# Head norms as one broadcast product, norm weights folded into rotary tables and splits

## The chip, the cores and the metric

The kernel runs on one core of a Trainium2 chip. The metric is the device time of one execution in microseconds; the figure for a kernel is the median of its runs. Besides the runs, one execution is recorded by the hardware profiler; its span runs from the first to the last instruction of the program. The core's engines are PE (matrix products), DVE (vector), ACT (scalar), POOL (GpSimd) and SP, which here only issues DMAs. Each engine executes its instructions strictly in the order in which the program lists them, and waits for others by semaphores.

## The reference

Two layers, each on 512 tokens of width 1024. A layer norms its input, multiplies it by one wide matrix, and hands the columns to four groups; their outputs are gated, joined, multiplied by `w_out` and added to the input. The change concerns two of the groups. In the first (latent attention) queries and keys come from low-rank projections that are themselves normed, and each head is normed again:

```
q = (rmsnorm(cq, mla_q_norm_g) @ mla_w_uq).reshape(B, S, MLA_HEADS, MLA_QK)
kv = (rmsnorm(ckv, mla_kv_norm_g) @ mla_w_ukv).reshape(B, S, MLA_HEADS, MLA_NOPE + MLA_V)
k_nope, v_a = kv[..., :MLA_NOPE], kv[..., MLA_NOPE:]
q = rmsnorm(q, mla_q_g)
q = jnp.concatenate([q[..., :MLA_NOPE], rope(q[..., MLA_NOPE:], positions)], axis=-1)
k_nope = rmsnorm(k_nope, mla_k_nope_g)
k_rope = rope(rmsnorm(kr, mla_k_rope_g)[:, :, None, :], positions)
```

There are 4 heads of 96 channels: 64 without position (`nope`), then 32 rotated ones. The ranks are 256 (`cq`) and 128 (`ckv`). In the second (block attention) both `mq` and `mk` are 4 heads of 64 channels, normed per head with `moba_q_g` and `moba_k_g`; their first 16 channels are rotated. A norm is `x * rsqrt(mean(x*x) + eps) * g`, a rotation is

```
x1, x2 = xf[..., :half], xf[..., half:]
return jnp.concatenate([x1 * cos - x2 * sin, x2 * cos + x1 * sin], axis=-1)
```

Both attentions use scores `q . k * scale` (scale 96^-0.5 and 64^-0.5) and a causal softmax.

## The kernel before

All products run in a form of float32 split in two: an operand is written as a rounded `hi` and the rest `lo` (`split2`, line 249: ACT copies `hi`, DVE subtracts to get `lo`), and a product is three matmuls (`mm3`, line 254). Tokens are four tiles of 128 rows.

The order of instructions on each engine is made by a planner in the kernel's own text (`Order`, line 67, and `Chain`, line 151). Every piece of work is a coroutine; each emitted instruction advances a clock of its engine by a cost formula, and the coroutine whose inputs come first by these clocks emits next. PE's clock is the planner's time. So a change of any instruction's cost or engine can move other instructions in the queues. The planner knows some DMAs (`dma`, line 262) and not others (the small parameter loads). `Slots` (line 113) hand out buffers; a coroutine waits for a free one.

What runs over what: `main` (line 1320), at the lowest priority, fills PE with the wide projection, first `cq` (the 416 columns of `cq`, `ckv`, `kr`) for the four tiles, then the units of `SEQ` (line 338) in order (`sq` with the columns of mq, then `ga`, `kv` with those of mk, `su`, `gc` and so on), and at last the output projection. Weights come in units: `load_units` (line 360) issues their loads on SP, `split_units` (line 378) splits each in two halves when PE is about to want it or when ACT and DVE are idle; it gives `hi` to DVE where ACT's clock is 600 ns ahead of DVE's.

The steps that the change and the prediction touch:

- `load_params` (line 528) loads 13 small parameter arrays of a layer on SP, each gain copied to all 128 partitions (`bcast`, line 511); its `scale` multiplies two of them on POOL by minus the score scale. For layer 0 it is called when the load of `ukv` has been issued (line 1536), for layer 1 from `next_params` (line 1265).
- `rope_tables` (line 445) computes cosine and sine of the positions on DVE or POOL, whichever is idle by the planner's clocks, at low priority, and sets `rope_ev`.
- `low_chain` (line 680), per tile: DVE multiplies the projected rows `a` by the low-rank gains `cg` into `ct` (line 687), PE transposes `ct` (`cT`), it is split (`cTh`, `cTl`), and PE forms `q` and `kv`. `low_stats` (line 650) takes the sums of squares on ACT meanwhile.
- `q_chain` (line 714) and `kv_chain` (line 743): copy to `Q` or `K`, four squares on ACT, POOL's power, then four DVE products, one per head, of rows times the head's factor times the gain; then Q is rotated (`rope`, line 635: six products and sums, on DVE or POOL, with one scratch tile `rb` for all rotations, so that these follow one another).
- `mqk_chain` (line 980) does the same for `mq` and `mk`.
- `mla_heads` (line 1132) starts when all tiles of `Q` and `K` are ready: per head PE transposes Q (`t0a`) and K (`t1a`), each is split (`hi0a`, `lo0a`, `hi1a`, `lo1a`), then scores, softmax, and product with V. `moba_heads` (line 1174) follows with pairs of heads (`mq0d`, `mk0d`, `kl0d` and so on).
- `sv_chain` (line 776) norms `vn`, which `mix_chain` (line 800) multiplies on PE (`mp`).
- `t_sums` (line 318) adds weight blocks in memory for the output projection by accumulating DMAs that POOL issues.

Of the kernel before, what the change touches and what calls it, by code (L numbers as in the profile page):

```python
# [11 lines left out]
F32 = mybir.dt.float32  # L12
# [188 lines left out]
def hybrid_trunk(ctx: ExitStack, tc: tile.TileContext, x, positions, norm_g, w_c, w_f, w_t, w_o, mla_q_norm_g,  # L201
# [176 lines left out]
    def split_units():  # L378
        for u in order:
# [3 lines left out]
            n = u.a * u.b  # L383
            for i in range(2):
# [142 lines left out]

    def load_params(L):
        l = L.l
        L.cg = lay.tile([P, 384], F32, tag="cg_b", name="cg_b")  # L530
        nc.sync.dma_start(L.cg[:, 0:256], dram(mla_q_norm_g, l * 256, [[0, P], [1, 256]]))
        nc.sync.dma_start(L.cg[:, 256:384], dram(mla_kv_norm_g, l * 128, [[0, P], [1, 128]]))
        L.gq = bcast(mla_q_g, l * 96, 96, "gq_b")
        L.gk = bcast(mla_k_nope_g, l * 64, 64, "gk_b")
# [3 lines left out]
        L.dq = bcast(moba_q_g, l * 64, 64, "dq_b")  # L538
        L.dk = bcast(moba_k_g, l * 64, 64, "dk_b")
# [8 lines left out]

        def scale():
            ch = Chain(o, L.par_t)  # L550
            yield from ch.pool(G.tensor_scalar, L.gq, L.gq, -(96 ** -0.5), None, op0=ALU.mult)
            yield from ch.pool(G.tensor_scalar, L.dq, L.dq, -0.125, None, op0=ALU.mult)
# [3 lines left out]
    for l in range(DEPTH):  # L556
        L = Layer()
        L.l = l
        L.ng_ev = Event()
# [75 lines left out]
    def rope(ch, x1, x2, cb, sb, nh, nd, name):  # L635
# [5 lines left out]
        for out_, in0, in1, op in ((ta, x2, sb, ALU.mult), (tb, x1, sb, ALU.mult), (x1, x1, cb, ALU.mult),  # L641
                                   (x2, x2, cb, ALU.mult), (x1, x1, ta, ALU.subtract), (x2, x2, tb, ALU.add)):
# [7 lines left out]
    def low_stats(L, t, a, t0, done):  # L650
# [24 lines left out]
        yield from rope(ch, krt[:, :, 0:16], krt[:, :, 16:32], cosT, sinT, 4, 16, f"k{L.l}")  # L675
# [4 lines left out]
    def low_chain(L, t, a, t0):  # L680
# [6 lines left out]
        yield from ch.dve(V.tensor_tensor, ct[:, :384], a[:, :384], L.cg, op=ALU.mult)  # L687
# [26 lines left out]
    def q_chain(L, t, q_ps, t0):  # L714
# [19 lines left out]
        for h in range(4):  # L734
            yield from ch.dve(V.scalar_tensor_tensor, Q[:, t, h, :], in0=Q[:, t, h, :], scalar=m[:, 4 + h:5 + h],
                              in1=L.gq, op0=ALU.mult, op1=ALU.mult)
        yield from ch.wait(rope_ev)
# [880 lines left out]
```

## Time and profile before

| | before |
|---|---|
| median of 3 runs | 497.65 us (497.48 to 499.13) |
| the profiled execution | 499.12 us, span 497.4 us |
| PE busy | 486.4 us, 98% of the span |
| DVE busy | 386.0 us, 78% |
| ACT busy | 317.0 us, 64% |
| POOL busy | 156.2 us, 31% |

Times in the profile are microseconds from the start of the span, unless they are marked or known as nanoseconds (mean time of one instruction of a group). A group is a line of the kernel, an engine, an operation, and output and input tiles with buffer numbers left out; as nearly all instructions are recorded at the planner's line 162 or 188, one goes by the tiles. After the bar stand busy time, mean of one, idle time of the engine just before, and what ended it. PE's instructions overlap, so the busy time of PE includes the end of one under the next; a 128x512 matmul follows the one before it after 0.23 us though it lasts 0.39.

### The profile page before, as it was taken

Reading aid. Unit: us, or ns where it says so; the run is one execution under the profiler, and the core shown is the slowest. Engines: PE = TensorE matmul, PEld = TensorE weight load, DVE = VectorE, ACT = ScalarE, POOL = GpSimd, SP = SyncE. Lnnn points to the kernel's source line nnn. Section 1 sums busy time; section 2 is a strip of 40 time slices with the busy share of each in tenths; the row PEclk is TensorE's granted clock in tenths of the full one; section 3 lists DMA queues with packets and bytes.
Section 4 is the critical chain, followed back from the end, with each engine's and each line's share of the span. In section 5 each row is a group of like instructions: output and inputs, shape, how many; then the busy total and the mean of one; then the engine's idle time right before and its main releaser. Section 6 shows DMA issues by size and latency. Waiting matters only on the chain.

```text
span 497.4 us, 7832 instructions
## 1 busy us (share of the span) xinstructions
PE 486.4 (98%) x2448; PEld 412.5 (83%) x2448; DVE 386.0 (78%) x1008; ACT 317.0 (64%) x933; POOL 156.2 (31%) x328
## 2 busy tenths in 40 slices
PE   6899999999999999999999999999999999999997
PEld 4798878788888888888889988888888888888886
DVE  4877884777988788669898698677969788765992
ACT  5688753576777775446657896567758587524640
POOL 6867883656110000000031388463351000000000
PEclk9999999999999999999999999999999999999999
DMA  8545559444575235786474232664548528565642
GB/s 273 150 141 199 196 117 203 171 86 88 192 145 188 71 98 175 210 299 219 157 256 157 86 106 108 211 149 97 118 122 245 142 102 215 174 249 188 227 171 92
DMA packets 35339, 81.98 MB, mean 165 GB/s; under 512 B 7137, under 2 KB 16609, under 8 KB 35042
## 3 DMA queue, kind: packets, MB, share of 16 engines
q1 hardware_dynamic: 26818, 73.10, 42.7%
q0 software_dynamic: 8480, 8.39, 11.5%
q8 instruction: 19, 0.31, 0.3%
q14 instruction: 22, 0.18, 0.1%
HBM read 73.61 MB, written 24.64 MB: 198 GB/s over the span
## 4 chain that ended last, share of the span: by engine, by line
PE 87%; POOL 4%; ACT 3%; DMA 3%; DVE 2%; issue 1%; POOLq 0%; DVEq 0%
PE kv L188 7%; PE cq L188 6%; PE oy L188 6%; PE sq L188 5%; PE cb L188 4%; PE gd L188 4%; PE ch L188 4%; PE cc L188 4%; PE su L188 4%; PE gc L188 4%; PE gb L188 4%; PE ox L188 4%; PE oz L188 4%; PE sa L188 3%; PE ga L188 2%; PE od L188 2%
## 5 line engine op out<-in xcount | busy, mean ns | idle before, releaser
L162 ACT ACTIVATE pd<-pd,mnd 128x256 f32<-128x256 f32 (+3 forms) x50 | 26.9, 547 | 2.8 <-DVE mnd L162 2.3
L330 POOL DMA_DIRECT2D t<-in_w_o_dram x16 | 17.9, 1121 | 33.1 <-DMA t<-t 22.6
L162 ACT ACTIVATE pha<-pTa 128x512 fp32r<-128x512 f32 (+3 forms) x32 | 13.9, 436 | 20.0 <-PE pTa L188 19.8
L188 PE MATMUL kv<-whi_kv,hTh 128*128 128x512 f32 x64 | 26.1, 408 | 0.0
L188 PE MATMUL kv<-whi_kv,hTl 128*128 128x512 f32 x64 | 25.1, 392 | 0.0
L188 PE MATMUL kv<-wlo_kv,hTh 128*128 128x512 f32 x64 | 25.0, 391 | 0.0
L188 PE MATMUL cq<-whi_c,hTh 128*128 128x416 f32 x64 | 24.0, 376 | 0.0
L162 ACT ACTIVATE phd<-pTd 128x512 fp32r<-128x512 f32 (+3 forms) x32 | 13.8, 434 | 14.9 <-PE pTd L188 14.7
L162 ACT ACTIVATE pa<-pa,mna 128x256 f32<-128x256 f32 (+3 forms) x40 | 21.4, 542 | 2.5 <-DVE mna L162 2.4
L188 PE MATMUL cq<-whi_c,hTl 128*128 128x416 f32 x64 | 22.6, 353 | 0.0
L188 PE MATMUL cq<-wlo_c,hTh 128*128 128x416 f32 x64 | 22.5, 351 | 0.0
L162 DVE TENSOR_TENSOR wlo_t<-raw_t,whi_t 128x512 fp32r<-128x512 f32 x32 | 21.1, 691 | 0.0
L162 ACT ACTIVATE whi_t<-raw_t 128x512 fp32r<-128x512 f32 x32 | 18.2, 618 | 4.1 <-DMA raw_t<-t 4.1
L162 POOL TENSOR_SCALAR xss<-xss 128x1 f32<-128x1 f32 x8 | 3.8, 476 | 52.3 <-ACT jk L162 45.1
L162 DVE TENSOR_TENSOR pla<-pTa,pha 128x512 fp32r<-128x512 f32 (+3 forms) x32 | 15.2, 484 | 5.5 <-ACT pha L162 5.5
L188 PE MATMUL sq<-yTh,hTh 128*128 128x512 f32 x48 | 18.9, 393 | 0.0
L188 PE MATMUL sq<-yTh,hTl 128*128 128x512 f32 x48 | 18.7, 390 | 0.0
L162 DVE TENSOR_TENSOR pld<-pTd,phd 128x512 fp32r<-128x512 f32 (+3 forms) x32 | 15.2, 484 | 4.5 <-ACT phd L162 4.4
L188 PE MATMUL sq<-yTl,hTh 128*128 128x512 f32 x48 | 18.7, 390 | 0.0
L162 DVE CUSTOM_DVE_ANT_0 pa<-sa,maskb 128x512 f32<-128x512 f32 (+3 forms) x32 | 14.8, 484 | 5.0 <-PE pTa L188 4.2
L162 DVE TENSOR_TENSOR wlo_b<-raw_b,whi_b 128x512 fp32r<-128x512 f32 x24 | 16.0, 688 | 0.7 <-ACT whi_b L162 0.7
L162 DVE CUSTOM_DVE_ANT_0 pd<-sd,maskb 128x256 f32<-128x256 f32 (+3 forms) x32 | 15.0, 483 | 2.0 <-PE pTd L188 1.9
(377 smaller groups left out, 1853.0 us busy)
## 6 DMA issues: line engine op xcount, KB each, us to landing
t<-in_w_o_dram POOLq DMA_DIRECT2D x16, 512.0 KB, 6.2
raw_t<-t SPq DMA_DIRECT2D x16, 512.0 KB, 4.0
raw_b<-in_w_o_dram SPq DMA_DIRECT2D x12, 512.0 KB, 4.2
raw_sq<-in_w_t_dram SPq DMA_DIRECT2D x8, 512.0 KB, 3.5
t<-in_w_o_dram SPq DMA_DIRECT2D x8, 512.0 KB, 4.4
raw_kv<-in_w_t_dram SPq DMA_DIRECT2D x8, 512.0 KB, 3.6
t<-t SPq DMA_DIRECT2D x8, 512.0 KB, 4.8
ys<-ysc SPq DMA_DIRECT2D x14, 256.0 KB, 5.2
```

Of the source, the lines that this page charges most:

```text
L162: f(*a, **k)
L188: f(*a, **k)
L330: nc.gpsimd.dma_start(z_src(l, n, j), quad(l, b, j), accum_op=ALU.add, max_dma_last_dim=1024)
```

## The change

- The four per-head products of each tile in `q_chain`, `kv_chain` and `mqk_chain` become one DVE product of the tile with the four factors, each repeated along its head; the gain is no longer in it.
- The gains of rotated channels go into four tables per kind (`tables`: cosine and sine times the gain of either half), made on POOL once per layer for Q, mq and mk. Rotation waits for its own table (`tab_ev`) in place of `rope_ev`.
- The gains of the other channels, of q and k together, and minus the score scale become one column per head dimension (`kac`, `kdc`), by which ACT and DVE multiply when transposed k is split. The split waits for `col_ev`.
- The low-rank gains become columns `cg`, applied where `uq` and `ukv` are split; those splits wait for `cg_ev`, and `hi` is always made on ACT. `ct` becomes a plain copy on ACT.
- `load_low_gain` issues the two loads of `cg`, in layer 0 right after the load of `c3` and ahead of the third and fourth tile of x. With them a layer has 18 small loads where it had 13 (six copied to all partitions for nine, six new ones of 64 numbers each).

```diff
@@ -381,6 +381,9 @@
             n = u.a * u.b
+            low = u.name[:-2] in ("uq", "ukv")
+            if low:
+                yield from ch.wait(layers[int(u.name[-1])].cg_ev)
             for i in range(2):
@@ -389,6 +392,13 @@
                 hi, lo, raw = u.hi[:, sl], u.lo[:, sl], u.raw[:, sl]
+                if low:
+                    k = i if u.a == 2 else 2
+                    col = layers[int(u.name[-1])].cg[:, k:k + 1]
+                    yield from c2.act(A.activation, hi, raw, AF.Copy, scale=col)
+                    yield from c2.dve(V.scalar_tensor_tensor, lo, in0=raw, scalar=col, in1=hi.bitcast(F32),
+                                      op0=ALU.mult, op1=ALU.subtract)
+                    continue
                 if o.clk["V"] + 600.0 < o.clk["A"]:
@@ -525,18 +535,29 @@
+    def load_low_gain(L):
+        L.cg = lay.tile([P, 4], F32, tag="cg", name="cg")
+        nc.sync.dma_start(L.cg[:, 0:2], dram(mla_q_norm_g, L.l * 256, [[1, P], [P, 2]]))
+        nc.sync.dma_start(L.cg[:, 2:3], dram(mla_kv_norm_g, L.l * P, [[1, P], [1, 1]]))
+        o.set(L.cg_ev, o.now + 4000.0)
+
     def load_params(L):
         l = L.l
-        L.cg = lay.tile([P, 384], F32, tag="cg_b", name="cg_b")
-        nc.sync.dma_start(L.cg[:, 0:256], dram(mla_q_norm_g, l * 256, [[0, P], [1, 256]]))
-        nc.sync.dma_start(L.cg[:, 256:384], dram(mla_kv_norm_g, l * 128, [[0, P], [1, 128]]))
-        L.gq = bcast(mla_q_g, l * 96, 96, "gq_b")
-        L.gk = bcast(mla_k_nope_g, l * 64, 64, "gk_b")
+        if l:
+            load_low_gain(L)
+        gq = bcast(mla_q_g, l * 96 + 64, 32, "gq_b")
         L.gr = bcast(mla_k_rope_g, l * 32, 32, "gr_b")
...
         L.lb = bcast(sg_ln_b, l * GW, GW, "lb_b")
-        L.dq = bcast(moba_q_g, l * 64, 64, "dq_b")
-        L.dk = bcast(moba_k_g, l * 64, 64, "dk_b")
+        dq = bcast(moba_q_g, l * 64, 16, "dq_b")
+        dk = bcast(moba_k_g, l * 64, 16, "dk_b")
+        L.ka = lay.tile([P, 2], F32, tag="ka", name="ka")
+        L.kd_ = lay.tile([P, 2], F32, tag="kd", name="kd")
+        for i, (a, b) in enumerate(((mla_q_g, moba_q_g), (mla_k_nope_g, moba_k_g))):
+            n = (96, 64)[i]
+            nc.sync.dma_start(L.ka[0:64, i:i + 1], dram(a, l * n, [[1, 64], [1, 1]]))
+            for r in range(2):
+                nc.sync.dma_start(L.kd_[r * 64:r * 64 + 64, i:i + 1], dram(b, l * 64, [[1, 64], [1, 1]]))
         L.sgb = lay.tile([P, 4], F32, tag="sgb", name="sgb")
@@ -546,17 +567,41 @@
+        def tables(ch, g, cs, sn, n, nm):
+
+            tab = lay.tile([P, 4, NT, n], F32, tag=f"tb{nm}", name=f"tb{nm}{l}")
+            for i, (w, h) in enumerate(((cs, 0), (sn, 1), (cs, 1), (sn, 0))):
+                yield from ch.pool(G.tensor_tensor, tab[:, i], w,
+                                   g[:, h * n:(h + 1) * n].unsqueeze(1).to_broadcast([P, NT, n]), op=ALU.mult)
+            L.tab[nm] = tab
+            o.set(L.tab_ev[nm], ch.t)
+
         def scale():
+
             ch = Chain(o, L.par_t)
-            yield from ch.pool(G.tensor_scalar, L.gq, L.gq, -(96 ** -0.5), None, op0=ALU.mult)
-            yield from ch.pool(G.tensor_scalar, L.dq, L.dq, -0.125, None, op0=ALU.mult)
+            yield from ch.wait(rope_ev)
+            yield from tables(ch, gq, cosT, sinT, 16, "q")
+            ce, se = (z.rearrange("p t (i two) -> p t i two", two=2)[:, :, :, 0] for z in (cosT, sinT))
+            yield from tables(ch, dq, ce, se, 8, "mq")
+            yield from tables(ch, dk, ce, se, 8, "mk")
+            L.kac = lay.tile([P, 1], F32, tag="kac", name="kac")
+            L.kdc = lay.tile([P, 1], F32, tag="kdc", name="kdc")
+            yield from ch.pool(G.memset, L.kac[64:96, :], -(96 ** -0.5))
+            yield from ch.pool(G.tensor_scalar, L.kac[0:64, :], L.ka[0:64, 0:1], L.ka[0:64, 1:2], -(96 ** -0.5),
+                               op0=ALU.mult, op1=ALU.mult)
+            yield from ch.pool(G.tensor_scalar, L.kdc, L.kd_[:, 0:1], L.kd_[:, 1:2], -0.125,
+                               op0=ALU.mult, op1=ALU.mult)
+            for r in (0, 64):
+                yield from ch.pool(G.memset, L.kdc[r:r + 16, :], -0.125)
+            o.set(L.col_ev, ch.t)
         o.spawn(scale(), None if L.l else MIXT, 2)
...
         L.l = l
-        L.ng_ev = Event()
+        L.ng_ev, L.cg_ev = Event(), Event()
+        L.tab, L.tab_ev, L.col_ev = {}, {n: Event() for n in ("q", "mq", "mk")}, Event()
         L.hT = [[Event(), Event()] for _ in range(NT)]
@@ -632,14 +677,14 @@
-    def rope(ch, x1, x2, cb, sb, nh, nd, name):
+    def rope(ch, x1, x2, c1, s2, c2, s1, nh, nd, name):
         tab = yield from rbS.get(ch, f"rb{name}")
...
         on_dve = o.clk["V"] + ROPEB < max(o.clk["G"], ch.t)
-        for out_, in0, in1, op in ((ta, x2, sb, ALU.mult), (tb, x1, sb, ALU.mult), (x1, x1, cb, ALU.mult),
-                                   (x2, x2, cb, ALU.mult), (x1, x1, ta, ALU.subtract), (x2, x2, tb, ALU.add)):
+        for out_, in0, in1, op in ((ta, x2, s2, ALU.mult), (tb, x1, s1, ALU.mult), (x1, x1, c1, ALU.mult),
+                                   (x2, x2, c2, ALU.mult), (x1, x1, ta, ALU.subtract), (x2, x2, tb, ALU.add)):
             if on_dve:
@@ -672,7 +717,7 @@
         yield from ch.wait(rope_ev)
-        yield from rope(ch, krt[:, :, 0:16], krt[:, :, 16:32], cosT, sinT, 4, 16, f"k{L.l}")
+        yield from rope(ch, krt[:, :, 0:16], krt[:, :, 16:32], cosT, sinT, cosT, sinT, 4, 16, f"k{L.l}")
         yield from ch.wait(L.QK_ev)
@@ -684,7 +729,7 @@
         o.spawn(low_stats(L, t, a, t0, done))
-        yield from ch.dve(V.tensor_tensor, ct[:, :384], a[:, :384], L.cg, op=ALU.mult)
+        yield from ch.act(A.activation, ct[:, :384], a[:, :384], AF.Copy)
         done(ch)
@@ -731,13 +776,11 @@
         yield from pow_rstd(ch, m[:, 4:8], m[:, 0:4], 4)
-        for h in range(4):
-            yield from ch.dve(V.scalar_tensor_tensor, Q[:, t, h, :], in0=Q[:, t, h, :], scalar=m[:, 4 + h:5 + h],
-                              in1=L.gq, op0=ALU.mult, op1=ALU.mult)
-        yield from ch.wait(rope_ev)
-        cb = cosT[:, t, :].unsqueeze(1).to_broadcast([P, 4, 16])
-        sb = sinT[:, t, :].unsqueeze(1).to_broadcast([P, 4, 16])
-        yield from rope(ch, Q[:, t, :, 64:80], Q[:, t, :, 80:96], cb, sb, 4, 16, f"q{t}{l}")
+        yield from ch.dve(V.tensor_tensor, Q[:, t], Q[:, t], m[:, 4:8].unsqueeze(2).to_broadcast([P, 4, 96]),
+                          op=ALU.mult)
+        yield from ch.wait(L.tab_ev["q"])
+        tabs = [L.tab["q"][:, i, t, :].unsqueeze(1).to_broadcast([P, 4, 16]) for i in range(4)]
+        yield from rope(ch, Q[:, t, :, 64:80], Q[:, t, :, 80:96], *tabs, 4, 16, f"q{t}{l}")
         o.set(L.qd[t], ch.t)
@@ -767,9 +810,8 @@
         yield from pow_rstd(ch, m[:, 4:8], m[:, 0:4], 4)
-        for h in range(4):
-            yield from ch.dve(V.scalar_tensor_tensor, K[:, t, h, 0:64], in0=K[:, t, h, 0:64],
-                              scalar=m[:, 4 + h:5 + h], in1=L.gk, op0=ALU.mult, op1=ALU.mult)
+        yield from ch.dve(V.tensor_tensor, K[:, t, :, 0:64], K[:, t, :, 0:64],
+                          m[:, 4:8].unsqueeze(2).to_broadcast([P, 4, 64]), op=ALU.mult)
         o.set(L.kd[t], max(ch.t, tv))
@@ -981,7 +1023,6 @@
             l = L.l
-            gn = L.dq if nm == "mq" else L.dk
             if t == 0:
@@ -995,14 +1036,11 @@
             yield from pow_rstd(ch, m[:, 4:8], m[:, 0:4], 4)
-            for h in range(4):
-                yield from ch.dve(V.scalar_tensor_tensor, dst[:, t, h, :], in0=dst[:, t, h, :],
-                                  scalar=m[:, 4 + h:5 + h], in1=gn, op0=ALU.mult, op1=ALU.mult)
-            yield from ch.wait(rope_ev)
-            ce = cosT[:, t, :].rearrange("p (i two) -> p i two", two=2)[:, :, 0]
-            se = sinT[:, t, :].rearrange("p (i two) -> p i two", two=2)[:, :, 0]
-            yield from rope(ch, dst[:, t, :, 0:8], dst[:, t, :, 8:16], ce.unsqueeze(1).to_broadcast([P, 4, 8]),
-                            se.unsqueeze(1).to_broadcast([P, 4, 8]), 4, 8, f"{nm}{t}{l}")
+            yield from ch.dve(V.tensor_tensor, dst[:, t], dst[:, t],
+                              m[:, 4:8].unsqueeze(2).to_broadcast([P, 4, 64]), op=ALU.mult)
+            yield from ch.wait(L.tab_ev[nm])
+            tabs = [L.tab[nm][:, i, t, :].unsqueeze(1).to_broadcast([P, 4, 8]) for i in range(4)]
+            yield from rope(ch, dst[:, t, :, 0:8], dst[:, t, :, 8:16], *tabs, 4, 8, f"{nm}{t}{l}")
             o.set(L.md_ev[nm][t], ch.t)
@@ -1149,7 +1187,14 @@
                 lo = yield from t2S.get(ch, f"lo{i}{H.name}", F32R)
-                yield from split2(ch, hi[:96], lo[:96], tp[:96])
+                if i == 0:
+                    yield from split2(ch, hi[:96], lo[:96], tp[:96])
+                else:
+                    yield from ch.wait(L.col_ev)
+                    col = L.kac[:96, :]
+                    yield from ch.act(A.activation, hi[:96], tp[:96], AF.Copy, scale=col)
+                    yield from ch.dve(V.scalar_tensor_tensor, lo[:96], in0=tp[:96], scalar=col,
+                                      in1=hi[:96].bitcast(F32), op0=ALU.mult, op1=ALU.subtract)
                 trS.put(ch)
@@ -1204,12 +1249,17 @@
                         pair[kind, x] = w
-                        yield from ch.act(A.activation, w[a0:a1, :], tp[a0:a1, :], AF.Copy)
-                        lo = w[b0:b1, :] if kind == "mq" else kl[a0:a1, :]
-                        if kind == "mk":
-                            yield from ch.act(A.activation, w[b0:b1, :], tp[a0:a1, :], AF.Copy)
-                        yield from ch.dve(V.tensor_tensor, lo, tp[a0:a1, :], w[a0:a1, :].bitcast(F32),
-                                          op=ALU.subtract)
+                        if kind == "mq":
+                            yield from ch.act(A.activation, w[a0:a1, :], tp[a0:a1, :], AF.Copy)
+                            yield from ch.dve(V.tensor_tensor, w[b0:b1, :], tp[a0:a1, :], w[a0:a1, :].bitcast(F32),
+                                              op=ALU.subtract)
+                        else:
+                            yield from ch.wait(L.col_ev)
+                            col = L.kdc[a0:a1, :]
+                            for r in (slice(a0, a1), slice(b0, b1)):
+                                yield from ch.act(A.activation, w[r, :], tp[a0:a1, :], AF.Copy, scale=col)
+                            yield from ch.dve(V.scalar_tensor_tensor, kl[a0:a1, :], in0=tp[a0:a1, :], scalar=col,
+                                              in1=w[a0:a1, :].bitcast(F32), op0=ALU.mult, op1=ALU.subtract)
                         o.set(pair["ev", x][0 if kind == "mq" else 1], ch.t)
@@ -1532,7 +1582,7 @@
         LOAD_HOOKS["c0_0"] = (after(1),)
-        LOAD_HOOKS["c3_0"] = (after(2), after(3))
+        LOAD_HOOKS["c3_0"] = (after(2), after(3), lambda: load_low_gain(L0))
         LOAD_HOOKS["ukv_0"] = (lambda: load_params(L0),)
...
         o.spawn(load_units(), None, 4)
```

## The prediction

> **What bounds the kernel now.** I read the sums first, then the chain that ended last, then busy time by stage.
>
> ```profile
> span 497.4 us, 7832 instructions
> PE 486.4 (98%) x2448; PEld 412.5 (83%) x2448; DVE 386.0 (78%) x1008; ACT 317.0 (64%) x933; POOL 156.2 (31%) x328
> PE 87%; POOL 4%; ACT 3%; DMA 3%; DVE 2%; issue 1%; POOLq 0%; DVEq 0%
> ```
>
> PE works 98% of the span and makes 87% of the chain. The change alters no matmul and no transpose, so it can win only where PE stands still, and lose only by making PE stand still. By stage (columns: length, busy time of PE, PEld, DVE, ACT, POOL with counts, clock, DMA share, GB/s):
>
> ```profile
> 12.50:25.00 12.50, 10.56 (x61) 9.54 (x60) 10.30 (x22) 8.47 (x27) 10.66 (x24) 1.00 0.54 153
> 25.00:37.50 12.50, 12.50 (x75) 11.91 (x74) 9.49 (x25) 10.93 (x41) 8.30 (x16) 1.00 0.44 137
> 37.50:50.00 12.50, 12.50 (x62) 10.91 (x61) 9.69 (x35) 10.91 (x51) 9.92 (x14) 1.00 0.50 201
> 62.50:75.00 12.50, 12.15 (x58) 9.82 (x58) 10.83 (x37) 7.45 (x28) 11.11 (x21) 1.00 0.53 108
> 87.50:100.00 12.50, 11.37 (x57) 9.39 (x56) 9.16 (x33) 6.70 (x30) 8.08 (x22) 1.00 0.46 169
> 275.00:287.50 12.50, 12.50 (x66) 11.35 (x66) 8.88 (x30) 10.94 (x54) 5.84 (x8) 1.00 0.23 84
> 287.50:300.00 12.50, 12.50 (x57) 10.43 (x57) 12.00 (x45) 11.70 (x55) 10.85 (x18) 1.00 0.41 128
> 487.50:497.40 9.90, 6.44 (x40) 5.64 (x38) 2.83 (x5) 0.00 (x0) 0.00 (x0) 0.98 0.26 95
> ```
>
> PE's idle time is 497.4 - 486.4 = 11.0 us. The rows hold 1.94 of it up to 25, 0.35 before 75, 1.13 before 100 and 3.46 at the end; in the slices left out PE is busy throughout but in the first, where the other 4.1 lie. The first and the last are loading, the norm of the first rows, and the last store; the change touches none of their steps. What it can reach:
>
> ```profile
> 20.20 0.34 PE L188 MATMUL cq<-whi_c,hTl 128*128 128x416 f32 x1
> 21.19 0.55 PE L188 MATMUL cT<-ident,ct 128*128 128x128 f32 x3 [0.64 <-DVE ct L162]
> 21.79 0.66 PE L188 MATMUL hT<-ident,h 128*128 128x128 f32 x4
> 71.36 0.38 PE L188 MATMUL mp<-vnh,wsh 128*128 128x256 f32 x1 [0.27 <-ACT vnh L162]
> 93.97 0.32 PE L188 MATMUL t0a<-ident,Q 128*96 128x128 f32 x1 [1.13 <-DVE Q L162]
> ```
>
> That is 0.64 + 0.35 (0.27 and 0.08 behind it) + 1.13 = **2.1 us**, the most that can be won. The other 1.3 us before 25 belong to the norm of the second 128 rows, untouched.
>
> **Head norms.** The four products per tile and the multiplication of `ct`, in all uses of both layers, then rows for what replaces them:
>
> ```profile
> L162 DVE SCALAR_TENSOR_TENSOR Q<-Q,mq,gq_b 128x96 f32<-128x96 f32 x32 | 10.2, 320 | 0.0
> L162 DVE SCALAR_TENSOR_TENSOR mq<-mq,mmq,dq_b 128x64 f32<-128x64 f32 x32 | 9.2, 299 | 1.4 <-POOL mmq L162 1.3
> L162 DVE SCALAR_TENSOR_TENSOR mk<-mk,mmk,dk_b 128x64 f32<-128x64 f32 x32 | 9.1, 288 | 0.4 <-POOL mmk L162 0.4
> L162 DVE SCALAR_TENSOR_TENSOR K<-K,mk,gk_b 128x64 f32<-128x64 f32 x32 | 8.6, 279 | 0.8 <-POOL mk L162 0.8
> L162 DVE TENSOR_TENSOR ct<-cq,cg_b x8: 545/550/563, 20.6 to 281.6; 128x384 f32<-128x384 f32 x8
> L162 DVE TENSOR_TENSOR wlo_uq<-raw_uq,whi_uq 128x384 fp32r<-128x384 f32 x2 | 1.1, 546 | 0.0
> L162 DVE TENSOR_TENSOR vnl<-vn,vnh 128x256 fp32r<-128x256 f32 x4 | 1.7, 421 | 0.6 <-ACT vnh L162 0.6
> L162 ACT ACTIVATE Q<-q x8: 471/482/501, 26.2 to 289.9; 128x384 f32<-128x384 f32 x8
> ```
>
> The 128 small products take 37.1 us of DVE. In their place come 8 of 128x384 (546 ns, by `wlo_uq`) and 24 of 128x256 (421 ns, by `vnl`): 4.4 + 10.1 = 14.5 us. No row shows a DVE product with one factor repeated along the innermost elements; between no extra cost and four separate passes the saving lies between 22.6 and 0 us, and I take 22.6, since the size of the operation set all those rows. `ct` leaves DVE (8 x 0.55 = 4.4 us) for ACT (8 x 0.48 = 3.9 us, by the equal copy `Q<-q`). So DVE loses 27 us, all under a PE that was busy anyhow. Worth to the time by itself: 0. If PE were not busy, it would be worth up to that.
>
> **What the move of `ct` wins.** Around PE's wait of 0.64 us:
>
> ```profile
> 18.80 0.51 ACT L162 ACTIVATE whi_uq<-raw_uq 128x384 fp32r<-128x384 f32 x1
> 21.17 0.20 ACT L162 ACTIVATE junk<-cq 128x32 f32<-128x32 f32 x1 [1.85 <-DVE ct L162]
> 19.92 0.75 DVE L162 SCALAR_TENSOR_TENSOR h<-x,xss,ng 128x512 f32<-128x512 f32 x1 [1.73 <-POOL xss L162]
> 20.58 0.55 DVE L162 TENSOR_TENSOR ct<-cq,cg_b 128x384 f32<-128x384 f32 x1
> 21.05 0.68 DVE L162 TENSOR_TENSOR hTl<-hT,hTh 128x512 fp32r<-128x512 f32 x1
> ```
>
> `ct` stood in DVE's queue behind `h`, which waited for POOL, while ACT stood idle 1.85 us. On ACT it can run from 19.3 and be done by 19.8, before PE asks at 20.4. What is late next is `hT` at 21.79, which (there are two PSUM buffers for transposes) waits for the one that `hTl` empties; `hTl` comes up by 21.05 - 20.58 = 0.47 us and no more, since `h` still ends near 20.66. Between 0 (the queue's order moves it back) and 0.64; I take **-0.45**.
>
> **The other two waits.** `mp` waits for `vn`, whose DVE products stand between the norms of mq; each tile's norm now holds DVE 0.42 us for some 0.9 before (four of 0.29, overlapping). Between 0 and 0.35: **-0.2**. `t0a` waits for the last rotary step of Q:
>
> ```profile
> 85.58 0.69 DVE L162 TENSOR_TENSOR wlo_su<-raw_su,whi_su 128x512 fp32r<-128x512 f32 x1 [5.33 <-ACT whi_su L162]
> 91.57 0.62 DVE L162 SCALAR_TENSOR_TENSOR mk<-mk,mmk,dk_b 128x64 f32<-128x64 f32 x1 [0.40 <-POOL mmk L162]
> 93.70 0.21 DVE L162 TENSOR_TENSOR Q<-Q,rbq 128x64 f32<-128x64 f32 x1
> 87.30 1.10 POOL L162 TENSOR_TENSOR rbk<-krt,sinT 128x64 f32<-128x64 f32 x2 [7.45 <-DVE Q L162]
> 89.49 0.60 POOL L162 TENSOR_TENSOR krt<-krt,rbk 128x64 f32<-128x64 f32 x2
> ```
>
> Between 91.57 and 93.91 four mk products are interleaved with Q's steps; one of 0.42 instead saves up to some 0.6. Against it stand the new tables: Q's rotation now waits for four POOL products of 128x64 after cosine and sine are ready. The same kind of row is 0.30 us each (`krt<-krt,rbk`, two in 0.60) up to 0.55 (`rbk`, two in 1.10): 1.2 to 2.2 us. They are covered if they fall into the 5.33 us that DVE stands idle, since the split of `raw_su` ahead of Q's later steps waits for its load; without that cover Q is late by 1.2 to 2.2 more. Bounds -1.13 and +2.2; I take **-0.1**.
>
> The Trainium skill (SBUF — State Buffer, section "SBUF: two separate sides") says that a DVE instruction with two SBUF inputs and a GpSimd one that reads SBUF lock a shared port pair against each other for a whole instruction. The two POOL rows above, same work at 0.30 and 0.55 us, agree. By it a broadcast product holds POOL out for 0.55 us at a time, not 0.32, and the tables would sit at the upper end; the sum would then be 1.0 us worse.
>
> **Parts costed at nothing.** The other POOL work (eight 128x32 products and some five small ones per layer) comes after Q's table; it delays K's split only through `col_ev`, some 8 x 0.3 + 5 x 0.3 = 4 us behind the tables, under the 5 serial rotations that use one scratch tile. Layer 1 makes its tables near 200 us, where POOL was idle. The split of transposed k and of the up-projections gets a scale by pointer:
>
> ```profile
> L162 ACT ACTIVATE Vt<-kv,ms x8: 454/468/497, 29.9 to 295.5; 128x256 fp32r<-128x256 f32 x8
> L162 ACT ACTIVATE K<-kv x8: 384/384/407, 28.1 to 288.9; 128x256 f32<-128x256 f32 x8
> 5.31 1.33 SPq L265 DMA_DIRECT2D x<-in_x_dram  x2
> 195.63 0.42 SPq L531 DMA_DIRECT2D cg_b<-in_mla_q_norm_g_dram  x1
> 204.30 0.41 SPq L265 DMA_DIRECT2D raw_b<-in_w_o_dram  x1
> 15.61 0.60 ACT L162 ACTIVATE hTh<-hT 128x512 fp32r<-128x512 f32 x1 [0.96 <-PE hT L188]
> ```
>
> 468 - 384 = 0.08 us more per ACT instruction; with 8 + 16 + 8 of them (k of the latent heads, k of the block heads twice, halves of up-projections) that is 2.7 us of ACT over the whole span, under busy PE; one in a head's preparation makes it 0.1 later. DVE's part of these splits changes from a difference (0.68, `hTl`) to a product and difference (0.75, `h`): 24 x 0.07 = 1.7 us, likewise covered. The new wait of those splits for `cg` on ACT holds `hTh` and the squares behind it, but `cg` is issued ahead of `raw_uq`, so it isn't last. SP issues 18 small loads per layer for 13. Two now stand before the third and fourth tile of x: 2 x 0.42 = 0.85 us later at issue. Landing shifts between 0 and 0.85; ACT has 0.96 us of idle ahead of `hTh` to take it: 0, without that cover +0.85. In layer 1 five more issues delay `raw_b` and what follows it by 5 x 0.42 = 2.1 us (the 13 took 195.63 to 204.30, so by 0.67 each 3.3 us), for weights of the output phase, which PE reaches at 216: 0.
>
> **Sum:** -0.45 - 0.2 - 0.1 = -0.75. The profiled execution took 499.12 (span 497.4, 1.7 around it) and would become 498.4. It is 1.47 above the median of the three runs, 497.65; on that footing the forecast is **496.9 us**, in its own range 496.3 to 498.0.
>
> **Rivals.** (1) *All of PE's reachable idle time goes*: 497.65 - 2.1 = 495.5. For it: DVE gets 27 us lighter and was at 10.83 of 12.5 before 75; the rotary tables may be ready sooner. Against: `t0a` hangs on `raw_su`'s landing, a DMA. 0.22.
> (2) *ACT becomes the bound* where `ct` lands on it. Before 50 us ACT was busy 10.93 and 10.91 of 12.5, from 275 to 300, just behind the copies of layer 1, 10.94 and 11.70. Four copies add 1.9 us to each stage, the pointers 0.3. From the point where less than 2.2 of ACT's 3.2 (layer 0) or 2.4 (layer 1) idle us can be filled, `hTh` and `cTh` come late and PE waits. One stage lost: 497.65 + 1.9 = 499.6; both: 501.5. Against: the scheduler gives the first half of a split to DVE when ACT runs 600 ns ahead. 0.20.
> (3) *The tables hit Q's rotation uncovered*, 1.2 to 2.2 us on `t0a`, less the first two gains: 498.2 to 499.2. 0.13.
> (4) *Nothing arrives*: the first gains are given back at `t0a`, because `raw_su`'s landing sets it: 497.6. 0.10.
>
> **How the numbers follow.** The forecast has 0.35. A measurement of this kernel can tell 0.3%, 1.5 us, from no change: faster is below 496.15, slower above 499.15. Faster: 0.20 of rival 1, 0.05 of the forecast: 0.25. Slower: 0.18 of rival 2, 0.07 of rival 3, 0.05 of the forecast by a new order of the queues: 0.30. Same: 0.45. The range goes from rival 1 (and 0.2 for the median's own spread) to one lost stage of rival 2 with the tables' extra: 495.3 to 500.0. It leaves out both lost stages (0.08) and, below, gains that no row explains (0.04).
>
> **What would show it.** Right: PE busy within 1 us of 486.4, `cT` without a wait near 20, DVE near 386 - 27 + 2 = 361 us, ACT near 317 + 4 + 3 = 324. The `t0a` wait between 0 and 1.2 would bear out the cover; over 2 would be rival 3. PE waits for `hTh`, `cTh` or `whi` between 25 and 50 or 275 and 300 would be rival 2. The forecast is wrong if PE's idle time moves by over 1.5 us, or if PE's own busy time grows.

## The result, and the profile after

The median after is 499.72 us in ten runs (499.2 to 502.37), against 497.89 us for ten runs of before (497.47 to 499.13) taken beside them. The ratio is 1.0046, 95% interval 1.0028 to 1.0065. (All ratios here are worked out over all runs of both kernels, the longer ones included; the two medians alone would give 1.0037.) The kernel became slower. The profiled execution of after took 499.20 us and is the fastest of the ten; what makes the others longer, up to 3 us, stands in no trace.

The sums of the page of after:

```profile
span 497.5 us, 7766 instructions
PE 487.3 (98%) x2448; PEld 412.2 (83%) x2448; DVE 375.6 (75%) x919; ACT 323.3 (65%) x941; POOL 160.1 (32%) x342
```

The stages of after (columns as in the prediction), with 300 to 312.5 added, since PE now stops there:

```profile
12.50:25.00 12.50, 11.13 (x66) 10.36 (x65) 10.42 (x20) 9.19 (x27) 10.54 (x25) 1.00 0.53 148
25.00:37.50 12.50, 12.38 (x73) 11.55 (x71) 10.14 (x29) 10.44 (x43) 9.25 (x15) 1.00 0.53 159
37.50:50.00 12.50, 12.50 (x61) 10.83 (x61) 8.85 (x28) 10.31 (x50) 7.49 (x12) 1.00 0.47 169
62.50:75.00 12.50, 11.28 (x54) 9.08 (x53) 9.17 (x23) 5.62 (x19) 11.61 (x21) 1.00 0.43 82
87.50:100.00 12.50, 12.50 (x62) 10.52 (x62) 7.35 (x24) 8.43 (x33) 5.57 (x15) 1.00 0.63 194
275.00:287.50 12.50, 12.50 (x66) 11.32 (x65) 9.75 (x29) 11.20 (x56) 7.68 (x11) 1.00 0.31 89
287.50:300.00 12.50, 12.50 (x57) 10.32 (x56) 9.60 (x36) 11.28 (x53) 7.17 (x10) 1.00 0.36 122
300.00:312.50 12.50, 11.94 (x58) 9.71 (x57) 9.96 (x31) 6.65 (x29) 10.30 (x19) 1.00 0.44 159
```

The two stages where PE lost, in a second profile of before (run b1 below):

```profile
62.50:75.00 12.50, 12.12 (x57) 9.72 (x57) 10.94 (x37) 7.26 (x27) 11.03 (x21) 1.00 0.52 121
300.00:312.50 12.50, 12.50 (x57) 10.36 (x56) 10.57 (x36) 6.78 (x28) 11.22 (x23) 1.00 0.32 103
```

PE stands idle 1.22 us for 0.38 around `mp`, and 0.56 for 0 around 309 us; from 12.5 to 25 it gained 0.57 (11.13 for 10.56). Nothing is lost from 37.5 to 50 or from 275 to 300, where ACT was nearly full in before; it is busy 10.31 us in the first of these stages and 11.28 in the last, less than before's 10.91 and 11.70. The three places on PE, after:

```profile
20.25 0.35 PE L188 MATMUL cq<-whi_c,hTl 128*128 128x416 f32 x1
20.43 0.49 PE L188 MATMUL cT<-ident,ct 128*128 128x128 f32 x3
21.04 0.66 PE L188 MATMUL hT<-ident,h 128*128 128x128 f32 x4
...
70.24 0.39 PE L188 MATMUL ga<-hTh,wlo_ga 128*128 128x512 f32 x1
71.77 0.38 PE L188 MATMUL mp<-vnh,wsh 128*128 128x256 f32 x1 [1.15 <-ACT vnh L162]
...
309.21 0.27 PE L188 MATMUL t0a<-ident,Q 128*96 128x128 f32 x1
310.04 0.53 PE L188 MATMUL t0a<-ident,Q 128*96 128x128 f32 x3 [0.56 <-POOL Q L162]
```

and in b1:

```profile
20.94 0.34 PE L188 MATMUL cq<-whi_c,hTl 128*128 128x416 f32 x1
...
71.38 0.39 PE L188 MATMUL ga<-hTh,wlo_ga 128*128 128x512 f32 x1
72.08 0.38 PE L188 MATMUL mp<-vnh,wsh 128*128 128x256 f32 x1 [0.30 <-ACT vnh L162]
...
93.44 0.60 PE L188 MATMUL t0a<-ident,Q 128*96 128x128 f32 x4
...
318.17 0.60 PE L188 MATMUL t0a<-ident,Q 128*96 128x128 f32 x4
```

From the last `cq` to `hT` pass 0.79 us; they were 1.59 in the rows of before (20.20 to 21.79), so the wait for `ct` is gone and 0.8 us won. From the last `ga` to `mp` pass 1.53 us for 0.70: 0.8 lost. In layer 1 `t0a` stands 45 matmuls earlier in PE's queue and comes 9 us earlier in the run; 0.83 us pass between its first tile and its second, for 0.11 in b1: 0.7 lost. In layer 0, the wait of 1.13 us at `t0a` is gone, but in b1, the unchanged kernel, it is gone as well.

The loss at `mp` is in good part the gain at `ct` given back. `mp` is PE's 312th matmul in both kernels, behind the same 311. What it waits for is `vnh`, a copy of `vn` by ACT, in b1 and then in after:

```profile
71.61 0.42 ACT L162 ACTIVATE vnh<-vn 128x256 fp32r<-128x256 f32 x1 [0.59 <-DVE vn L162]
...
71.30 0.42 ACT L162 ACTIVATE vnh<-vn 128x256 fp32r<-128x256 f32 x1 [1.21 <-DVE vn L162]
```

Counted from the last `cq` (20.94 in b1, 20.25 in after), the last `ga` starts at 49.99 us in after for 50.44, so PE comes 0.45 sooner, while `vnh` starts at 51.05 for 50.67, 0.38 later. In a second profile of after (a1 below) PE comes 0.74 sooner and `vnh` 0.07 later. PE waits out at `mp` what it won at `ct`, because `vnh` hangs on POOL and DVE. From the same `cq` to the end of the span b1 takes 475.85 us, after 477.25 and a1 477.29: 1.4 more. Of this, 0.4 has come up where `mp` starts (0.1 in a1), 0.7 comes at `t0a` of layer 1, and in a1 0.5 at `t0a` of layer 0; the rest is spread over small differences.

Why Q is late at 309: the last of its rotation, on POOL in after.

```profile
306.49 1.01 POOL L162 TENSOR_TENSOR mmq<-mmq,nhalf 128x4 f32<-128x4 f32 x1
...
308.21 0.77 POOL L162 TENSOR_TENSOR Q<-Q,rbq 128x64 f32<-128x64 f32 x1
309.07 0.52 POOL L162 TENSOR_SCALAR bmv<-bmv 128x1 f32<-128x1 f32 x1
309.67 0.32 POOL L162 TENSOR_TENSOR Q<-Q,rbq 128x64 f32<-128x64 f32 x1
```

The rotation shares POOL with the norms of mq and vn; its last step ends at 309.99, and PE had reached it at 309.21. PE's queue was written by the planner, whose prices put `t0a` this early.

### The profile page after: what moved, and what is told of

Read it like the earlier page. It is cut to its first block, busy times and chain, and to the rows that moved or that the text cites. A ratio compares the mean times of both kernels' runs of the same rounds, so it can differ in the third digit from the quotient of the medians.

```text
span 497.5 us, 7766 instructions
## 1 busy us (share of the span) xinstructions
PE 487.3 (98%) x2448; PEld 412.2 (83%) x2448; DVE 375.6 (75%) x919; ACT 323.3 (65%) x941; POOL 160.1 (32%) x342
## 4 chain that ended last, share of the span: by engine, by line
PE 85%; POOL 8%; ACT 3%; DVE 2%; issue 1%; DMA 1%; POOLq 0%; DVEq 0%
PE kv L188 10%; PE oy L188 6%; PE cq L188 5%; PE cb L188 4%; PE ch L188 4%; PE gb L188 4%; PE gd L188 4%; PE cc L188 4%; PE gc L188 4%; PE su L188 4%; PE oz L188 4%; PE ox L188 4%; PE sa L188 3%; PE ga L188 3%; PE oa L188 2%; PE od L188 2%
## 5 line engine op out<-in xcount | busy, mean ns | idle before, releaser
L162 ACT ACTIVATE pa<-pa,mna 128x256 f32<-128x256 f32 (+3 forms) x43 | 22.9, 547 | 2.6 <-DVE mna L162 2.5
L162 DVE TENSOR_TENSOR pld<-pTd,phd 128x512 fp32r<-128x512 f32 (+3 forms) x32 | 15.2, 484 | 5.1 <-ACT phd L162 5.1
L162 ACT ACTIVATE whi_b<-raw_b 128x512 fp32r<-128x512 f32 x23 | 13.7, 622 | 7.3 <-DMA raw_b<-in_w_o_dram 7.3
```

What stands on the lines that cost most here:

```text
L162: f(*a, **k)
```

## The experiments

Theory A: the gain of 0.8 at `ct` is real, but the lighter plan moves `mp` and the heads forward in PE's order, ahead of chains that the plan thinks faster than they are. (In after this doesn't hold of `mp` in layer 0, as its place in the queue shows.) Rivals: the added work costs (R); any new order costs, wherever (B, later O). Wherever runs are compared, it is with runs of before on the same chip; the medians of before were 497.79, 497.87, 497.99 and 498.24 us in the four batches.

**b1, a1: the two kernels profiled again, unaltered.**

> The kernel before, unchanged, profiled once more. The profiled execution that the prediction rests on took 499.12 us, at the upper end of that kernel's ten runs (median 497.89). Theory A (the forecast subtracted from waits that a typical run lacks): about 497.6 us, span about 495.9, and PE's wait of 1.13 us ahead of the last t0a transpose near 93 us is under 0.3. Rival (the waits are always there and the rest of the difference lies outside the span): span 497.4 again, t0a wait 0.8 to 1.3.

> The changed kernel, unchanged, profiled once more; its ten runs lie at 499.2 to 499.9 or at 501.0 to 502.4. Theory A: the PE waits of the first profile are steady, ahead of mp near 71 us 0.9 to 1.3 and ahead of t0a near 310 us 0.4 to 0.8; time 499.2 to 499.9. If the run is one of those above 501, its 2 to 3 us are one or two further PE waits at a place where a weight load or an accumulating DMA lands late. Rival: the waits differ from run to run and no place repeats.

b1 took 498.49 us without the wait at `t0a`; a1 took 499.73, with `mp` 1.52 us behind `ga`, `t0a` of layer 1 stopped again (309.67, then 310.49), and 0.38 us of waiting at `t0a` of layer 0 (94.45). So the two new waits stand in both profiles of after, and the one in layer 0 comes and goes with either kernel. The order of the queues is the same in both profiles of a kernel.

**b_lat, a_lat: another order without another instruction.** The planner's latency between engines, in before and in after:

```diff
-LAT, PELAT, SLACK, PEMARGIN = 130.0, 220.0, 300.0, 80.0
+LAT, PELAT, SLACK, PEMARGIN = 134.0, 220.0, 300.0, 80.0
```

> The kernel before with one constant of the planner changed (latency between dependent instructions 130 to 134 ns), so the same instructions in a slightly other order. Theory B (any new order costs, the change's parts do not): 498.9 to 500.5, that is 1.0 to 2.5 us over before, with new PE waits. Theory A (the change's own parts cost): within 0.7 us of before, 497.2 to 498.6.

> The changed kernel with the same constant changed from 130 to 134 ns. Theory B: its time scatters about that of b_lat, anywhere from 497 to 501, and the waits ahead of mp and t0a move or vanish. Theory A: 499.2 to 500.5 with the wait ahead of mp near 71 us still 0.8 or more.

b_lat: 498.95 us, ratio 1.0019 (1.0008 to 1.0029), with a new wait of 0.87 us inside `mp` at 73.08. a_lat: 500.15 us, 1.0055 (1.0035 to 1.0074), with 0.85 at `hT` (28.60), 0.95 at a later `mp` (74.63), and `t0a` of layer 1 still stopped (309.77, then 310.59). A change of 4 ns in the plan is worth 1 us in before; for after it moves waits and takes none off the sum. In these runs, and in all below but bn_same, the plan also gives some 15 to 55 of the 7,800 instructions to another engine.

**b_norms: the broadcast products alone in before.** In `q_chain`, and likewise in the other two chains:

```diff
-        for h in range(4):
-            yield from ch.dve(V.scalar_tensor_tensor, Q[:, t, h, :], in0=Q[:, t, h, :], scalar=m[:, 4 + h:5 + h],
-                              in1=L.gq, op0=ALU.mult, op1=ALU.mult)
+        yield from ch.dve(V.tensor_tensor, Q[:, t], Q[:, t], m[:, 4:8].unsqueeze(2).to_broadcast([P, 4, 96]),
+                          op=ALU.mult)
```

> The kernel before with one part of the change alone: the four scalar_tensor_tensor of each head norm become one broadcast product; the head gains (gq, gk, dq, dk) are left out of the output; ct, the rotary tables, the splits and the loads stay as before. Theory A (what costs is where the lighter DVE plan puts the heads in PE's order, with POOL's powers and rotations now last): this part alone brings new steady PE waits, between 0.5 and 1.3 us at t0a of layer 1 or at mp, and the time is 498.3 to 499.5, ratio 1.001 to 1.003. Rival R (what costs is the work that the other parts add: tables on POOL, gains on ACT and DVE in the splits, 5 more loads): 497.0 to 497.9, ratio 0.998 to 1.000.

502.44 us, ratio 1.0084 (1.0069 to 1.01): slower than the whole change, and than either theory expected. PE's timeline:

```profile
72.08 0.38 PE L188 MATMUL mp<-vnh,wsh 128*128 128x256 f32 x1 [1.34 <-ACT vnh L162]
...
313.82 0.38 PE L188 MATMUL mp<-vnh,wsh 128*128 128x256 f32 x1 [1.20 <-ACT vnh L162]
```

Neither the tables nor the gains in the splits nor the new loads are in this kernel, so R falls as the main cause. The wait at `mp` now stands in both layers.

**a_plan: after, its plan charged as for four small products.**

```diff
+        o.clk["V"] += 4 * 61 + 3 * (68 + LAT)
+        ch.t += 4 * 61 + 3 * (68 + LAT)
```

> The kernel after, its planner charged for each broadcast product what it charged for the four small ones (838 ns more on DVE's planned clock and on the chain); the same instructions, another order. Theory A: PE's heads go back to about where before had them, the wait of 0.8 us at t0a of layer 1 near 309 us is gone and that of 1.3 at mp falls below 0.6; with cT's wait gone as in after, 497.5 to 498.4, ratio 0.9995 to 1.0015. Rival R (the added work costs): the time stays at 499.2 to 500.2, ratio 1.003 to 1.005. Rival B (any new order costs about 0.2 per cent against the order that the constants were tuned for): 498.7 to 499.5 with new waits at other places.

501.26 us, 1.008 (1.0051 to 1.0108): a miss. Both waits that it was aimed at are gone, but others came: 0.90 at `t0a` in layer 0 (99.15), and the largest at a transpose in the softmax of the block heads:

```profile
185.17 0.44 PE L188 MATMUL pTd<-ident,pd 128*128 128x128 f32 x2 [2.17 <-DVE kl1d L162]
```

The plan also gave POOL some steps of the angles and rotations that DVE had. In this order a part of the output comes out wrong, from a cause that is not known; the run counts for its order's time alone. It speaks for O.

**a_pow4, a_pow300, b_pow4, bn_pow4: POOL's price.** A power of four elements costs 960 ns in the plan; in after the four groups of them measure 1113 to 1252 ns on the mean, and in before, with the same price, 1082 to 1223. With 1340 ns (in after, before and b_norms), and 1500 (300 for 260, in after):

```diff
-        return self._emit("G", 300 + 165 * free_size(a[0]), f, a, k)
+        return self._emit("G", 300 + (260 if free_size(a[0]) == 4 else 165) * free_size(a[0]), f, a, k)
```

> The kernel after, the planner's price of a POOL power of 4 elements raised from 960 to 1340 ns (they measure 1111 to 1252 on the mean); the same instructions, another order. Theory A: the plan now has PE reach mp and t0a of layer 1 after POOL's chain, both waits below 0.5 us, 497.8 to 498.8, ratio 1.000 to 1.002. Rival R: 499.2 to 500.2, ratio 1.003 to 1.005. Rival B: 498.7 to 499.5, new waits elsewhere.

a_pow4: 497.48 us, 0.9991 (0.9982 to 1.0). Around both places:

```profile
71.23 0.39 PE L188 MATMUL ga<-hTh,wlo_ga 128*128 128x512 f32 x1
71.46 0.28 PE L188 MATMUL mp<-vnh,wsh 128*128 128x256 f32 x1
...
311.51 0.38 PE L188 MATMUL mp<-vnl,wsh 128*128 128x256 f32 x1 [0.29 <-DVE vnl L162]
...
312.90 0.60 PE L188 MATMUL t0a<-ident,Q 128*96 128x128 f32 x4
```

`mp` follows `ga` without a gap, `t0a` of layer 1 comes 3.7 us later and runs through. In layer 0 `mp` is PE's 312th matmul here too: not PE's order but a sooner `vnh` takes that wait away. `vnh` starts 48.66 us behind the last `cq`, for 51.05 in after.

> The kernel after with the power's price at 1500 ns in place of 960 (1340 gave 497.48). Theory A2: any price above what the powers take keeps PE behind POOL: waits at mp and at t0a of layer 1 below 0.5 us, 497.0 to 498.8, ratio 0.998 to 1.002. Rival O: the 1340 was a lucky draw; this price gives 499 to 501 with waits elsewhere.

497.94 us, 0.9992 (0.9983 to 1.0001), neither wait there: the price need not be hit exactly.

> The kernel before with the broadcast head norms alone (the head gains left out of the output) and the power's price at 1340 ns. Theory A2: both waits of 1.85 and 1.7 us at mp go below 0.6 each and the time falls from 502.44 to 497.5 to 499.0, ratio 1.000 to 1.002. Rival O: it stays above 500, ratio above 1.004, or new waits as long stand elsewhere.

497.97 us, 1.0001 (0.999 to 1.0013), 4.5 us less than b_norms with both `mp` waits gone. As A expected.

> The kernel before with the planner's price of a POOL power of 4 elements raised from 960 to 1340 ns; nothing else. Theory A2 (the lighter DVE plan lets PE arrive ahead of POOL's late powers; the cure is POOL's price): before already lives with small waits, so it gains little: 496.9 to 498.2, ratio 0.998 to 1.001, and the changed kernel with the same price (497.48) is then no more than 0.3 per cent better. Rival S (the price's gain has nothing to do with the change): before gains as much as after did, 0.4 per cent or more, 495.0 to 495.9. Rival O (any new order is a draw): slower than before by 0.2 to 0.5 per cent, with waits at other places.

499.83 us, 1.0035 (1.0023 to 1.0047): S falls, since the price helps only the kernels with the broadcast products, but so does A's figure. The wait at `mp` of layer 0 goes; PE waits 1.44 us at `oy` near 243 instead. That is O's outcome, in one profile.

**a_ctdve: `ct` back on DVE in after.**

```diff
-        yield from ch.act(A.activation, ct[:, :384], a[:, :384], AF.Copy)
+        yield from ch.dve(V.tensor_scalar, ct[:, :384], a[:, :384], 1.0, None, op0=ALU.mult)
```

> The kernel after with the copy of ct put back on DVE (a multiplication by 1.0 there in place of ACT's plain copy); all else as after but for the order that the planner makes of it. If the copy on ACT removed cT's wait of 0.64 to 0.80 us near 21 us, the wait comes back with 0.4 to 0.8 us, ratio 1.005 to 1.006 (500.0 to 500.8). If the wait went for another reason (DVE freed by the head norms and by the splits), it stays away and the ratio stays at 1.004 to 1.005.

500.93 us, 1.0055 (1.0043 to 1.0068). The wait is back:

```profile
19.90 0.34 PE L188 MATMUL cq<-whi_c,hTl 128*128 128x416 f32 x1
20.55 0.55 PE L188 MATMUL cT<-ident,ct 128*128 128x128 f32 x3 [0.30 <-DVE ct L162]
```

`cT` follows 0.65 us behind the last `cq`, for 0.18 in after and 0.99 before: so the move to ACT takes 0.47 of the 0.8. The rest is neither the move nor the head norms, none of which has run by then. `h`, ahead of `ct` in DVE's queue, waits 1.28 us for POOL's `xss` here and in after, for 1.73 in before. POOL's steps up to there are the same in the same order, but one of them took less; in before and then here:

```profile
17.65 0.77 POOL L162 TENSOR_SCALAR rope_scratch<-rope_scratch 128x64 f32<-128x64 f32 x1
...
17.35 0.37 POOL L162 TENSOR_SCALAR rope_scratch<-rope_scratch 128x64 f32<-128x64 f32 x1
19.27 0.75 DVE L162 SCALAR_TENSOR_TENSOR h<-x,xss,ng 128x512 f32<-128x512 f32 x1 [1.28 <-POOL xss L162]
```

It took 0.76 us in b1, and 0.37 in after and a1. Beside it DVE begins its split of `raw_uq`, which now multiplies by the gain; whether that is the cause isn't shown. The time of a_ctdve has a new order in it, too (a wait of 1.23 us at `mp` of layer 1), and isn't used as a price.

**a_qdve: Q always rotated on DVE.**

```diff
-        on_dve = o.clk["V"] + ROPEB < max(o.clk["G"], ch.t)
+        on_dve = name[0] == "q" or o.clk["V"] + ROPEB < max(o.clk["G"], ch.t)
```

> The kernel after with the rotation of Q always on DVE (in after the planner puts 2 of 8 tiles there), power's price as in after. Theory A2 (POOL is last at the heads): t0a's wait of 0.8 us near 309 us goes below 0.3, and the waits at mp fall, since POOL has some 8 us less; 498.0 to 499.2, ratio 1.000 to 1.003. Rival D (the wait is Q's chain itself, whoever runs it): t0a waits for DVE at the same place by 0.5 us or more, 499.2 to 500.5.

502.98 us, 1.0108 (1.0077 to 1.0139), longer than either theory expected. (In after four of the eight tiles are rotated on DVE, not two.) `t0a` of layer 1 runs through, but in layer 0 it now waits for DVE, and `mp` still waits 1.14:

```profile
92.78 0.32 PE L188 MATMUL t0a<-ident,Q 128*96 128x128 f32 x1 [2.06 <-DVE Q L162]
```

That POOL alone is last at these places, as A2 had it, falls.

**bn_same: the broadcast products alone, in before's order.** The planner steps through four calls as before, of which only the first emits an instruction:

```diff
+            yield from ch._emit("V", 129 + 1.047 * 96, NOOP if h else V.tensor_tensor,
+                                (Q[:, t], Q[:, t], m[:, 4:8].unsqueeze(2).to_broadcast([P, 4, 96])), {"op": ALU.mult})
```

> The kernel before with the broadcast head norms alone (head gains left out of the output), the planner charged call by call as for the four small instructions: TensorE, ACT, POOL and SP get their instructions in exactly before's order, and only DVE's are fewer. Theory A2 (the order costs, the lighter work does not): not slower than before, 497.2 to 498.0, ratio 0.9985 to 1.0005; mp's wait near 71 us no longer than before's 0.5 to 0.8 (both steps), t0a of layer 1 without a wait. Rival W (the broadcast products themselves cost, by their length or by holding POOL off): slower, ratio 1.002 to 1.008, with b_norms' waits of 1.5 us or more at mp.

498.48 us against 498.24, ratio 1.0001 (0.9985 to 1.0017). The page's sums and PE's timeline:

```profile
PE 486.5 (98%) x2448; PEld 412.5 (83%) x2448; DVE 373.4 (75%) x912; ACT 317.2 (64%) x933; POOL 158.7 (32%) x328
```

```profile
72.02 0.39 PE L188 MATMUL mp<-vnh,wsh 128*128 128x256 f32 x1 [0.29 <-ACT vnh L162]
...
318.27 0.60 PE L188 MATMUL t0a<-ident,Q 128*96 128x128 f32 x4
```

The trace has PE's 2448, ACT's 933 and POOL's 328 instructions in exactly before's order. It is the same work as b_norms, with 0.29 at `mp` as in b1 (0.30) and `t0a` at b1's place. W falls. This settles it for the norms: with the order held, they cost and bring nothing beyond the interval's 0.8 us; the 0.84% of b_norms is the order's, with the 40 or so instructions that the plan moves between engines. The tables, the splits and the loads were not run with the order held. That they need not cost is shown by a_pow4 and a_pow300, which have all of them.

**a_ts0: an accumulating DMA moved.** In after POOL issues one between the two steps of the last variance of vn:

```profile
67.78 0.19 POOL L162 TENSOR_SCALAR bmv<-bmv 128x1 f32<-128x1 f32 x1
68.04 1.20 POOL L330 DMA_DIRECT2D t<-in_w_o_dram  x1
68.86 1.01 POOL L162 TENSOR_TENSOR bmv<-bmv,nhalf 128x1 f32<-128x1 f32 x1
```

```diff
-TS0 = 36000.0
+TS0 = 39000.0
```

> The kernel after with TS0 at 39000 in place of 36000: POOL issues the accumulating DMA behind the last tile's power of bmv, no longer between its two steps; PE's order changes little ahead of mp. If that issue (1.2 us) makes most of mp's wait, the 1.31 us there falls to 0.3 or less and the time to 498.5 to 499.2, ratio 1.001 to 1.003. If the plan's early place for mp makes it, the wait stays above 0.8 and the ratio at 1.003 to 1.005.

501.15 us, 1.0059 (1.0037 to 1.008). The power ends at 68.71 where it ended at 69.87, the plan puts `vn`'s first product ahead of the second split of `raw_kv` on DVE, and `vnh` came 0.6 us sooner; but the plan also took three matmuls of `ga` from ahead of `mp`, and PE came 0.6 sooner too:

```profile
69.65 0.39 PE L188 MATMUL ga<-hTh,wlo_ga 128*128 128x512 f32 x1
71.17 0.38 PE L188 MATMUL mp<-vnh,wsh 128*128 128x256 f32 x1 [1.13 <-ACT vnh L162]
```

The wait is the same, but only because both sides of it moved by 0.6 us. So the DMA and the split did hold `vnh`, and the run doesn't part them from PE's place; a new wait of 1.18 us at `hT` (262.49) is in its time as well. What stands ahead of `vn` in after's DVE queue:

```profile
69.51 0.77 DVE L162 TENSOR_TENSOR wlo_kv<-raw_kv,whi_kv 128x512 fp32r<-128x512 f32 x1 [0.45 <-ACT whi_kv L162]
70.20 0.47 DVE L162 SCALAR_TENSOR_TENSOR vn<-sq,bmv,lg_b 128x256 f32<-128x256 f32 x1
70.78 0.48 DVE L162 SCALAR_TENSOR_TENSOR vn<-vn,bmv,lb_b 128x256 f32<-128x256 f32 x1
```

DVE waits there for ACT's half of a weight split, and `vn`, whose power is done at 69.87, waits behind it until 70.20.

**All runs together.** With POOL's old price and the order left to the planner, the seven kernels with the broadcast products lie from 1.0046 to 1.0108; the three with a raised price lie from 0.9991 to 1.0001. That is more than O alone would lead one to expect, but the three share one edit, and A's own figure for before failed. That the order makes the loss is shown; whether it is POOL's price or any order but the tuned one stays open.

## Why the prediction was wrong

- **The step that failed** is the treatment of the queues' order as given, with the waits as terms that add up. The prediction counted PE's existing waits as all that could change, and let "a new order of the queues" cost 0.05 of the chance. The planner writes a new order of every queue for any change: the runs that edit the plan alone lie from 0.9991 to 1.0080 of before, and bn_same, in the old order, lies at 1.0001. In the sum's terms: `ct` gave -0.8 (forecast -0.45), `mp` +0.8 (forecast -0.2), since PE came sooner and `vnh` did not, and `t0a` of layer 1, which was no term at all, +0.7. From `ct` to the end of the span, after's two profiles take 1.4 us more than b1. The medians lie 1.8 apart; the other 0.4 is in executions that were not profiled, and stays open.
- **A term that was not there.** The sum worked on the 1.13 us at `t0a` of layer 0, and rival 1 on all of it. b1 shows that it is no property of the kernel.
- **`ct`: right as far as it goes.** Forecast -0.45; the rows give -0.8, of which `ct`'s place on ACT makes 0.47, the size that was forecast. The rest came because `h` did not end where the prediction left it (near 20.66): it ends at 20.39 in after, behind the POOL step that took 0.37 us for 0.77. Of the 0.8, the two profiles of after wait out 0.45 and 0.74 again at `mp`.
- **The signs could not tell.** PE's busy time went from 486.4 to 487.3 us, which is within 1 us (right) and has grown (wrong), and its idle time fell from 11.0 to 10.2 while the kernel became slower. b1, the unchanged kernel, has 488.1 and 8.7.
- **The loads ahead of x, put at nothing: right.** The last `cq` starts at 20.25 and 20.70 us in the two profiles of after, and at 20.20 and 20.94 in those of before.
- **DVE's saving was sized wrongly, the single costs rightly.** The products in after:

```profile
L162 DVE TENSOR_TENSOR Q<-Q,mq 128x384 f32<-128x384 f32 x8 | 4.6, 576 | 1.3 <-POOL mq L162 1.3
L162 DVE TENSOR_TENSOR mq<-mq,mmq 128x256 f32<-128x256 f32 x8 | 3.6, 450 | 2.3 <-POOL mmq L162 2.2
L162 DVE TENSOR_TENSOR mk<-mk,mmk 128x256 f32<-128x256 f32 x8 | 3.5, 442 | 1.7 <-POOL mmk L162 1.6
L162 DVE TENSOR_TENSOR K<-K,mk 128x256 f32<-128x256 f32 x8 | 3.5, 434 | 1.9 <-POOL mk L162 1.9
```

  15.2 us, where 14.5 were forecast: the repeated factor costs nearly nothing, which no row had shown. But the engine's busy time falls only from 386.0 in before to 373.4 in bn_same, 13 us and not 22: the small products overlap with each other and with their neighbours in DVE's queue, so their durations add up to more than their time. b1 shows two of them, 0.25 and 0.28 long, in 0.45:

```profile
68.24 0.27 DVE L162 SCALAR_TENSOR_TENSOR mq<-mq,mmq,dq_b 128x64 f32<-128x64 f32 x1
68.52 0.45 DVE L162 SCALAR_TENSOR_TENSOR mq<-mq,mmq,dq_b 128x64 f32<-128x64 f32 x2
```

  Hence 375.6 in after where 361 were forecast. ACT's 323.3 agrees with 324. That a lighter DVE is worth 0 by itself under a busy PE was right: bn_same, within 0.8 us.
- **Rivals.** ACT as the bound (2) fell as a mechanism: at most 0.12 us of idle PE from 25 to 50 and none from 275 to 300. That its 499.6 is close to the time is luck, and so is that the time lies in the range. The tables on Q's rotation (3): they end at 76.59 us in after, ahead of Q's first rotation at 77.35, so they were covered; `t0a` of layer 0 waits 0 and 0.38 us in two profiles, for rotations some 16 us later, and not the 1.2 to 2.2. Rival 4 had the gains given back, but at `t0a` for a load; they were given back at `mp` for `vnh`. The four products that make Q's tables took 0.55 us and three times 0.32 in layer 0, and 0.32 to 0.77 in layer 1; the 1.0 us of loss did not come in layer 0. By the Trainium skill's rule of the shared port pair, which a DVE instruction with two SBUF inputs and a GpSimd instruction take from each other for a whole instruction (SBUF — State Buffer, section "SBUF: two separate sides"), they would sit at their upper end. The spread of 0.32 to 0.77 would agree with that rule, but no run here parts it from other causes. "Slower" held 0.30 of the chance, 0.25 of it for reasons that did not come true and 0.05 for the one that did, a new order of the queues.

## What to carry to other kernels

Where a planner writes the queues, a change to any cost is also a change of order; price that by the scatter of edits to the plan alone (here -0.1 to +0.8%), and test the work by itself with the order held, by charging the plan as before. In a kernel whose main engine is 98% busy, ask of every relief which engine's plan becomes the optimistic one, and compare its prices with the measured durations before reading the result: 380 ns more on POOL's powers turned 1.0046 into 0.9991. Profile the unchanged kernel twice before counting a wait as there to be won. And before adding a gain to the sum, ask for the next wait behind it: what that wait hangs on decides whether the gain is kept.

## What the runs showed of the hardware that was not expected

A DVE product whose second factor is repeated along the innermost 96 or 64 elements takes 576 ns for 128x384 and 434 to 450 for 128x256, against 550 for a plain product of the first size (`ct` in before) and 421 for a plain difference of the second (`vnl`). A POOL power of 128x1 takes 0.58 us in a_ts0 and 1.01 in after, where the profile lets it begin under the issue of a DMA (1.20 us) that it follows.
